# A hybrid attention and retention layer on one core: query loads of the attention's first half from ScalarE's DMA queue

## Chip, cores and metric

The kernel runs on one core of one Trainium2 chip. The metric is the time of one execution on the device in microseconds (us), as a median of runs. The core's engines are TensorE (PE, whose weight loads are listed apart as PEld), VectorE (DVE), ScalarE (ACT), GpSimd (POOL) and SyncE (SP, which computes nothing here and issues DMAs). Each takes its own stream of instructions in order; they wait for each other on semaphores.

## What is computed

One layer of a streaming encoder, for 2048 new frames of a prompt and 64 frames of a running stream with 4096 past ones. Per frame, an RMS norm and one wide input projection feed two branches: a differential attention (four heads, each query and key split into two halves of 64, causal by chunks of 64 frames) and a retention with a decaying state. Gates merge the branches and an output projection follows. The part that matters here is the attention over the prompt:

```python
def diff_attention(q, k, v, q_pos, k_pos, lam, slopes):
    s = jnp.einsum('bqhcd,bkhcd->bhcqk', q, k).astype(jnp.float32) * (DK_A ** -0.5)
    dist = jnp.abs(q_pos[:, None] - k_pos[None, :]).astype(jnp.float32)
    s = s - slopes[None, :, None, None, None] * dist[None, None, None]
    allowed = (k_pos[None, :] // CHUNK) <= (q_pos[:, None] // CHUNK)
    s = jnp.where(allowed[None, None, None], s, -jnp.inf)
    p = jax.nn.softmax(s, axis=-1)
    a = p[:, :, 0] - lam * p[:, :, 1]
    return jnp.einsum('bhqk,bkhe->bqhe', a.astype(v.dtype), v)
```

## The kernel before

**A planner writes the order.** The kernel is written as generators, one per task: the input projection's columns (`w_stream`), the attention's heads, the retention, the output. A loop (`loop`) resumes the ready task of the highest priority, and keeps an estimated clock for each engine: `P`, `A`, `V` and `G` add the estimated cost of a PE, ACT, DVE or POOL instruction to that engine's clock and return the time at which its result is there. A task that needs a result yields that time and is resumed when PE's clock has come to it. So the order in which instructions are issued to PE, ACT and DVE, and which of them stand next to each other, follows from these estimates: a changed estimate deals the order anew from that place on. The three engines keep this order as written; SP's and POOL's streams are ordered by the framework from the same program.

**Loads.** `ld` issues a DMA on SP's queue and returns an estimated landing time; `st` does the same for a store. Every DMA of the program takes one of eight semaphores, named DMAHW0_49 to DMAHW7_49 in the rows below, in turn, whichever queue it is on. Before a DMA is issued, its engine waits until the DMA that had the same semaphore, eight places earlier in the program, has landed.

**The attention.** It runs in two halves: query blocks 0 to 3 of 256 frames for all four heads, then blocks 4 to 7. For head `h` and block `p`, `load_q` fetches the query block: a buffer of 128 partitions x 4 x 256 floats (two buffers exist) is filled by four DMAs of 128 KB, one for each of the two terms (high and low part) and each half of the partitions. `q_loader` walks through heads and blocks; `load_head` fetches the keys (`K`) and values (`V`) of a head, and for the very first head also issues the first two query loads. `qk_block` makes the scores of 128 queries against the keys seen so far: two matmuls per 512 columns into a PSUM bank (L1582, L1583), which DVE moves to SBUF with the distance term added and a maximum taken (L1591, `a_acc`). `softmax` takes exponentials on ACT (L1622) and combines the two halves on DVE (L1644). `at_pv` transposes the rows on PE (L1694), casts the result to a high part on ACT (`ath`, L1708), subtracts it on DVE to get the low part (`atl`, L1710), and multiplies both with the values (L1672 to L1674). A query buffer is given back when the last score matmul of its block has run.

**What runs beside it.** The attention does not run alone: the projection's matmuls (`mm_group`, L1039) fill PE between its steps, and the retention runs beside both. A weight tile `ws` of the projection is loaded, cast on ACT (`wh`, L993) and split on POOL (`wl`, L1003). When a group of the value columns is done, ACT casts it into the buffer `thi` (L1287) and copies it to `raw` (L1289), DVE makes `tlo`, and three stores (L271) take them out. There is one buffer for `thi`, so the next such cast waits until the store of the one before has landed. Copies of other columns to `ev` (L1356) are stored to `qbT` and the like.

Of the kernel before, what the change touches and what calls it, by code (L numbers as in the profile page):

```python
# [8 lines left out]
F32 = mybir.dt.float32  # L9
# [154 lines left out]
class Hybrid:  # L164
# [97 lines left out]
        self.pool = max(self.pool, ready) + 2.4 * n + 100  # L262
        return self.pool + LAT

    def ld(self, dst, src, nbytes=0):
        self.nc.sync.dma_start(dst, src)
        self.dma = max(self.dma, self.pe) + nbytes / 300.0
        return self.dma + DMA_LAT

# [1240 lines left out]
    def load_q(self, h, p):  # L1510
        t0 = 256 * p
        yield from self.take("q")
        q = self.sb(self.ap, [128, 4, 256], "q", dt=F32R)
        for j in range(2):
            qj = self.qT[j][h, :, t0:t0 + 256].rearrange("(c d) t -> d c t", c=2)
            for o in (0, 64):
                t = self.ld(q[o:o + 64, 2 * j:2 * j + 2].bitcast(F32), qj, 1 << 17)
        self.qs.append((q, t))

    def q_loader(self, half):  # L1520
# [1374 lines left out]
```

## Time and profile before

| what | value |
|---|---|
| median of 3 runs | 1894.08 us (1893.97 to 1894.23) |
| the profiled execution's own time | 1897.48 us |
| its span, first to last instruction | 1895.5 us |
| mean granted PE clock | 0.999 |
| query loads: DMA issues, size, median to landing | 128, 128 KB, 3.7 us |
| of these in the attention's first half | 64, issued from 598.7 to 832.2 us |

The profile is of one execution, a little longer than the runs without a profile. In its lists of groups and waits an engine's name is followed by the kernel's line and by the tiles written and read; "SPq" is SyncE's queue of DMA issues, and the time of such a row is that of the issue, not of the transfer. "PE busy" includes matmuls that overlap each other, so what PE loses is best read from the waits. A DMA share of 1 means that the core's 16 DMA engines were busy all the time.

### The profile page before, as it was taken

To read this page: it belongs to the slowest core of one execution; us is meant where nothing else is said; L and a number is where in the kernel's file an instruction comes from. 1 tells how busy PE (TensorE), PEld (TensorE's weight loads), DVE (VectorE), ACT (ScalarE), POOL (GpSimd) and SP (SyncE) were. 2 spreads that over 40 slices of the span, in tenths; PEclk is the share of its full clock that TensorE was granted. 3 is DMA by queue.
4 is the path that set the end of the run, shared out by engine and by line. 5 is a ranking of instruction groups with operands and counts; after the bars stand their busy time and mean duration, and the time that the engine had idled before them with its cause. 6 is when DMAs were issued, how large, how long until landed. Compare 5 with 4: busy or idle time off the path is not lost.

```text
span 1895.5 us, 32109 instructions
## 1 busy us (share of the span) xinstructions
PE 1877.3 (99%) x10970; PEld 1649.7 (87%) x10970; DVE 1267.2 (67%) x2994; ACT 955.9 (50%) x2217; POOL 590.8 (31%) x557
## 2 busy tenths in 40 slices
PE   9999999999999899999999999999999999999999
PEld 7788888888888789888888899999999999999887
DVE  6765856657575667877577776687873329977664
ACT  6434654454434566455556555566664436654221
POOL 2420356555643132031211112211113526522442
PEclk9999999999999999999999999999999999999999
DMA  7654555565566785565523444734414748876542
GB/s 255 213 175 124 169 169 165 168 193 180 179 181 187 222 233 157 143 204 135 160 73 105 137 120 119 203 85 116 116 52 127 227 133 261 269 237 205 174 157 77
DMA packets 360581, 313.01 MB, mean 165 GB/s; under 512 B 67937, under 2 KB 310241, under 8 KB 360418
## 3 DMA queue, kind: packets, MB, share of 16 engines
q1 hardware_dynamic: 360418, 310.97, 56.0%
q8 instruction: 86, 1.41, 0.3%
q14 instruction: 77, 0.63, 0.1%
HBM read 205.43 MB, written 104.60 MB: 164 GB/s over the span
## 4 chain that ended last, share of the span: by engine, by line
PE 65%; DMA 2%; SPq 1%; DVE 1%; ACT 0%; issue 0%; POOL 0%; DVEq 0%; POOLq 0%; ACTq 0%
PE mm L1039 26%; PE at L1694 3%; PE s L1582 2%; PE s L1583 2%; PE pv L1674 2%; PE pv L1673 2%; PE pv L1672 2%; PE s L2496 1%; PE s L2498 1%; PE s L2497 1%; PE mm L2372 1%; PE at L2373 1%; PE s L2372 1%; PE s L2373 1%; PE at L2372 1%; PE s L2374 1%
## 5 line engine op out<-in xcount | busy, mean ns | idle before, releaser
L1003 POOL TENSOR_TENSOR wl<-ws,wh 128x512 fp32r<-128x512 f32 x125 | 172.5, 1396 | 360.5 <-ACT wh L993 271.8
L1039 PE MATMUL mm<-xh,wh 128*128 128x256 f32 (+2 forms) x784 | 258.4, 330 | 0.0
L1039 PE MATMUL mm<-xh,wl 128*128 128x256 f32 (+2 forms) x784 | 254.4, 324 | 0.0
L1039 PE MATMUL mm<-xl,wh 128*128 128x256 f32 (+2 forms) x784 | 254.2, 324 | 0.0
L1039 PE MATMUL mm<-wh,xh 128*128 128x512 f32 x504 | 203.3, 403 | 0.0
L1039 PE MATMUL mm<-wh,xl 128*128 128x512 f32 x504 | 197.8, 392 | 0.0
L1039 PE MATMUL mm<-wl,xh 128*128 128x512 f32 x504 | 197.6, 392 | 0.0
L1622 ACT ACTIVATE row<-row,a_mx 128x1024 f32<-128x1024 f32 (+7 forms) x144 | 149.6, 1041 | 16.4 <-DVE a_mx L1601 16.4
L1039 PEld LDWEIGHTS mm<-xh,wl 128*128 128x128 f32 x784 | 148.1, 189 | 10.3 <-POOL wl L1003 0.5
L1039 PEld LDWEIGHTS mm<-xh,wh 128*128 128x128 f32 x784 | 148.2, 189 | 9.9
L1039 PEld LDWEIGHTS mm<-xl,wh 128*128 128x128 f32 x784 | 148.4, 189 | 9.6
L1710 DVE TENSOR_TENSOR atl<-at,ath 128x512 fp32r<-128x512 f32 (+1 forms) x144 | 92.5, 659 | 80.4 <-ACT ath L1708 80.0
L1448 POOL TENSOR_TENSOR r_y<-r_y,r_sq 128x256 f32<-128x256 f32 x32 | 27.7, 865 | 360.1 <-DVE r_sq L1445 193.3
L1708 ACT CAST ath<-at 128x512 fp32r<-128x512 f32 (+1 forms) x144 | 79.4, 565 | 105.8 <-PE at L1694 103.5
L1591 DVE CUSTOM_DVE_ANT_0 row<-s,dfar 128x512 f32<-128x512 f32 (+2 forms) x150 | 93.2, 635 | 52.5 <-PE s L1583 47.6
L768 POOL TENSOR_TENSOR wl<-ws,wh 128x256 fp32r<-128x256 f32 x64 | 57.5, 899 | 190.7 <-ACT wh L759 187.1
L1039 PEld LDWEIGHTS mm<-wh,xl 128*128 128x128 f32 x504 | 94.7, 188 | 21.3
L1039 PEld LDWEIGHTS mm<-wh,xh 128*128 128x128 f32 x504 | 94.8, 188 | 17.4 <-DVE tlo L1291 0.2
L1039 PEld LDWEIGHTS mm<-wl,xh 128*128 128x128 f32 x504 | 95.0, 188 | 17.0
L1644 DVE SCALAR_TENSOR_TENSOR row<-row,a_w 128x1024 f32<-128x1024 f32 (+5 forms) x88 | 98.9, 1131 | 0.0
L993 ACT CAST wh<-ws 128x512 fp32r<-128x512 f32 x128 | 76.9, 621 | 38.6 <-DMA ws<-in_w_in_dram 25.8
L1582 PE MATMUL s<-K,q 128*128 128x512 f32 (+3 forms) x244 | 93.2, 384 | 1.3 <-DVE a_acc L1591 1.0
(497 smaller groups left out, 5441.3 us busy)
## 6 DMA issues: line engine op xcount, KB each, us to landing
ws<-in_w_in_dram SPq DMA_DIRECT2D x160, 256.0 KB, 3.5
q<-qT SPq DMA_DIRECT2D x128, 128.0 KB, 3.7
K<-kT SPq DMA_DIRECT2D x48, 256.0 KB, 4.3
V<-vN SPq DMA_DIRECT2D x24, 512.0 KB, 5.2
row<-in_x_prompt_dram SPq DMA_DIRECT2D x16, 512.0 KB, 4.4
wz<-in_w_in_dram SPq DMA_DIRECT2D x32, 256.0 KB, 4.3
row<-in_cache_k_T_dram SPq DMA_DIRECT2D x32, 256.0 KB, 3.5
row<-in_cache_v_diff_dram SPq DMA_DIRECT2D x32, 256.0 KB, 3.1
```

Of the source, the lines that this page charges most:

```text
L768: nc.gpsimd.tensor_sub(l[:, cs], src, h[:, cs].bitcast(F32))
L993: self.nc.scalar.copy(h, st)
L1003: self.nc.gpsimd.tensor_sub(l, st, h.bitcast(F32))
L1039: nc.tensor.matmul(ps, p, q, start=c == 0 and i == 0, stop=c == KC - 1 and i == 2)
L1582: nc.tensor.matmul(ps, q1s, kk, start=True, stop=False)
L1591: nc.vector.tensor_tensor_reduce(out=row[:, k0:k0 + n], in0=ps, in1=tab, scale=-SLOPES[h], scalar=3.0e38, op0=ALU.add, op1=ALU.min, accum_ ...
L1622: nc.scalar.activation(u, u, AF.Exp, bias=mx, scale=-1.0, accum_out=lp[:, k:k + 1])
L1644: nc.vector.scalar_tensor_tensor(out=u0, in0=u1, scalar=w[:, 0:1], in1=u0, op0=ALU.mult, op1=ALU.add)
L1694: nc.tensor.transpose(at[:, w:w + 128], src, self.ident)
L1708: nc.scalar.copy(ah[:, :w], at[:, :w])
L1710: nc.vector.tensor_sub(al[:, :w], at[:, :w], ah[:, :w].bitcast(F32))
L2372: nc.tensor.matmul(ps, wh[:, u, csl], oh, start=kt == 0, stop=False)
```

## The change

`ld` takes a queue, and `load_q` passes ScalarE's for blocks 0 to 3, that is for the attention's whole first half, and SyncE's for blocks 4 to 7. For each of the moved DMAs the planner's ACT clock is set to at least PE's and advanced by 165 + 435 = 600 ns.

```diff
--- before.py
+++ after.py
@@ -262,8 +262,8 @@
         self.pool = max(self.pool, ready) + 2.4 * n + 100
         return self.pool + LAT
 
-    def ld(self, dst, src, nbytes=0):
-        self.nc.sync.dma_start(dst, src)
+    def ld(self, dst, src, nbytes=0, queue=None):
+        (queue or self.nc.sync).dma_start(dst, src)
         self.dma = max(self.dma, self.pe) + nbytes / 300.0
         return self.dma + DMA_LAT
 
@@ -1511,10 +1511,13 @@
         t0 = 256 * p
         yield from self.take("q")
         q = self.sb(self.ap, [128, 4, 256], "q", dt=F32R)
+        queue = self.nc.sync if p > 3 else self.nc.scalar
         for j in range(2):
             qj = self.qT[j][h, :, t0:t0 + 256].rearrange("(c d) t -> d c t", c=2)
             for o in (0, 64):
-                t = self.ld(q[o:o + 64, 2 * j:2 * j + 2].bitcast(F32), qj, 1 << 17)
+                t = self.ld(q[o:o + 64, 2 * j:2 * j + 2].bitcast(F32), qj, 1 << 17, queue)
+                if p < 4:
+                    self.A(0, self.pe, 435)
         self.qs.append((q, t))
 
     def q_loader(self, half):
```

The number of instructions of every kind stays the same on PE, DVE and POOL; ACT has 64 DMA issues more and SP 64 fewer. Since the planner's estimates change with the first moved load, the order on PE, ACT and DVE differs from there until about the last quarter of PE's stream, which is the same again. Behind the change's added lines the numbers are higher by 3: L1582 is L1585, L1622 is L1625, L1708 is L1711.

Three places follow. In the rows, `[waits ...]` names the semaphores that the instruction waits for.

SyncE, where the attention begins: `K`, `V` and `q` are keys, values and queries, `dfar` is a table of distances, `ws` a weight tile, `qbT<-ev` a store. Before:

```order
L266 DMA q<-qT_58 64x2x256 [waits DMAHW0_49]
L266 DMA q<-qT_58 64x2x256 [waits DMAHW1_49]
L271 DMA qbT<-ev 128x256 [waits DMAHW2_49,Activation_49]
L266 DMA ws<-in_w_in_dram 128x512 [waits DMAHW3_49,Pool_49]
L266 DMA q<-qT_57 64x2x256 [waits DMAHW4_49]
L266 DMA q<-qT_57 64x2x256 [waits DMAHW5_49]
L266 DMA q<-qT_58 64x2x256 [waits DMAHW6_49]
L266 DMA q<-qT_58 64x2x256 [waits DMAHW7_49]
L266 DMA ws<-in_w_in_dram 128x512 [waits DMAHW0_49,Pool_49]
L266 DMA dfar<-in_c_dfar_dram 128x1920 [waits DMAHW1_49]
L266 DMA V<-vN_61 128x8x128 [waits DMAHW2_49]
L266 DMA V<-vN_62 128x8x128 [waits DMAHW3_49]
```

and with the change:

```order
L266 DMA K<-kT_60 64x1024 [waits DMAHW3_49]
L266 DMA ws<-in_w_in_dram 128x512 [waits DMAHW6_49,Pool_49]
L266 DMA ws<-in_w_in_dram 128x512 [waits DMAHW7_49,Pool_49]
L271 DMA qbT<-ev 128x256 [waits DMAHW0_49,Activation_49]
L266 DMA dfar<-in_c_dfar_dram 128x1920 [waits DMAHW1_49]
L266 DMA V<-vN_61 128x8x128 [waits DMAHW2_49]
L266 DMA V<-vN_62 128x8x128 [waits DMAHW3_49]
```

The query loads are gone from between `ws`, `qbT`, `dfar` and `V`; the eight semaphores still go round over both queues.

ScalarE, some instructions later, about the third query load. Before:

```order
L993 COPY wh<-ws 128x512 [waits DMAHW3_49,PE_49,Pool_49] x2
L1622 ACTIVATE row,a_lp<-row,a_acc 128x128 [waits DVE_49] x2
L993 COPY wh<-ws 128x512 [waits DMAHW0_49,PE_49,Pool_49]
L1622 ACTIVATE row,a_lp<-row,a_acc 128x256 [waits DVE_49] x2
L1622 ACTIVATE row,a_lp<-row,a_acc 128x384 [waits DVE_49]
L1356 COPY ev<-mm 128x320 [waits DMAHW4_49,PE_49,Activation_49]
L1622 ACTIVATE row,a_lp<-row,a_acc 128x384 [waits DVE_49]
L993 COPY wh<-ws 128x512 [waits DMAHW0_49,Pool_49]
```

and with the change:

```order
L993 COPY wh<-ws 128x512 [waits PE_49,Pool_49]
L993 COPY wh<-ws 128x512 [waits DMAHW6_49,PE_49,Pool_49]
L1625 ACTIVATE row,a_lp<-row,a_acc 128x128 [waits DVE_49] x2
L266 DMA q<-qT_57 64x2x256 [waits DMAHW7_49,DMAHW3_49,PE_49]
L266 DMA q<-qT_57 64x2x256 [waits DMAHW1_49]
L266 DMA q<-qT_58 64x2x256 [waits DMAHW3_49]
L266 DMA q<-qT_58 64x2x256 [waits DMAHW5_49]
L1625 ACTIVATE row,a_lp<-row,a_acc 128x256 [waits DVE_49]
L993 COPY wh<-ws 128x512 [waits DMAHW7_49,PE_49,Pool_49]
L1625 ACTIVATE row,a_lp<-row,a_acc 128x384 [waits DVE_49]
L1356 COPY ev<-mm 128x320 [waits DMAHW4_49,PE_49,Activation_49]
L1625 ACTIVATE row,a_lp<-row,a_acc 128x256
```

The four DMAs of the third load stand between the exponentials of the first pair of query blocks. The second waits on DMAHW1, which `dfar` had, the third on DMAHW3, which the second `V` load had, and the fourth on DMAHW5, which a store `qbT<-ev` had. On PE, between the first score matmul and the first that needs the third load, there stood five groups of three 512-wide projection matmuls and three groups of three 320-wide ones; now there stand three of the former and four of the latter.

ScalarE, about the first casts of attention rows. Before:

```order
L1708 COPY ath<-at 128x384 [waits PE_49]
L1287 COPY thi<-mm 128x512 [waits PE_49]
L1289 COPY raw<-mm 128x512 [waits DMAHW6_49,DMAHW5_49]
L1622 ACTIVATE row,a_lp<-row,a_mx 128x640 [waits DVE_49,Activation_49]
L1404 COPY r_o<-pv 128x256 [waits PE_49]
L1406 ACTIVATE r_sq<-r_o 128x256 [waits Activation_49]
L1408 ACTIVATE r_hi<-r_o 128x256
L1622 ACTIVATE row,a_lp<-row,a_mx 128x640 [waits DVE_49]
L1622 ACTIVATE row,a_lp<-row,a_mx 128x768 [waits DVE_49]
L1287 COPY thi<-mm 128x512 [waits DMAHW4_49,PE_49]
L1289 COPY raw<-mm 128x512 [waits DMAHW7_49]
L1708 COPY ath<-at 128x512 [waits PE_49]
```

and with the change:

```order
L266 DMA q<-qT_58 64x2x256 [waits DMAHW1_49]
L1287 COPY thi<-mm 128x512 [waits PE_49]
L1289 COPY raw<-mm 128x512 [waits DMAHW7_49]
L1625 ACTIVATE row,a_lp<-row,a_mx 128x640 [waits DVE_49]
L1625 ACTIVATE row,a_lp<-row,a_mx 128x768 [waits DVE_49,Activation_49]
L266 DMA q<-qT_57 64x2x256 [waits DMAHW4_49,DMAHW5_49,DMAHW3_49,PE_49]
L266 DMA q<-qT_57 64x2x256 [waits DMAHW6_49]
L266 DMA q<-qT_58 64x2x256 [waits DMAHW0_49]
L266 DMA q<-qT_58 64x2x256 [waits DMAHW2_49]
L1711 COPY ath<-at 128x384 [waits PE_49]
L1625 ACTIVATE row,a_lp<-row,a_mx 128x768 [waits DVE_49]
L1287 COPY thi<-mm 128x512 [waits DMAHW5_49,PE_49,Activation_49]
```

The first `ath` (128x384) stood ahead of both `thi`; it now stands behind one of them and behind the fourth and fifth query loads (of the fourth, its last DMA is the first row here), and ahead of the second `thi`. The second pair's `ath` (128x512), which stood right behind the second `thi` and `raw`, now stands behind the third.

## The prediction

> **What bounds the kernel now.** I read the page first, then the busy time by stage, then the weight loads' waits in the stage that the change touches, then the chain of waits there.
>
> ```profile
> span 1895.5 us, 32109 instructions
> PE 1877.3 (99%) x10970; PEld 1649.7 (87%) x10970; DVE 1267.2 (67%) x2994; ACT 955.9 (50%) x2217; POOL 590.8 (31%) x557
> ```
>
> TensorE (PE) is busy 99% of the span; its work is the same before and after, so the change can only move the few microseconds in which PE waits. Where these lie is shown by the busy time in stretches (columns: stretch, its length, busy time of PE, of weight loads, VectorE, ScalarE, GpSimd, granted clock, DMA share, GB/s):
>
> ```profile
> 598.00:700.00 102.00, 94.09 (x559) 82.73 (x559) 57.19 (x184) 52.63 (x134) 18.64 (x15) 0.98 0.86 236
> 700.00:800.00 100.00, 100.00 (x652) 90.77 (x651) 77.82 (x245) 58.69 (x151) 18.59 (x17) 1.00 0.56 157
> 800.00:900.00 100.00, 100.00 (x592) 88.30 (x591) 77.45 (x221) 57.42 (x141) 21.35 (x18) 1.00 0.60 171
> ```
>
> The moved loads are issued between 598.7 and 832.2 us. In that stretch PE idles 7.9 us (102.00 - 94.09), all of it before 700; from 700 to 900 it idles 0. What a weight load (PEld) waited for in 598 to 700 us (total us, times, longest):
>
> ```profile
> PEld pv L1672 <- ACT ath L1708: 3.1, 1, 3.1
> PEld tp L1582 <- issue: 2.9, 1, 2.9
> PEld s L1582 <- DVE a_acc L1591: 1.3, 2, 0.8
> PEld pv L1674 <- DVE atl L1710: 1.3, 2, 0.7
> PEld s L1583 <- DMA q<-qT: 0.8, 1, 0.8
> PEld tp L1583 <- DMA q<-qT: 0.7, 1, 0.7
> ```
>
> That is 10.1 us in all, in two large stalls. The chain of waits from 596 to 640 us says what each stands on (start us, us, what):
>
> ```profile
> 606.67 1.30 SPq L266
> 608.02 7.59 DMA V<-vN
> 615.63 0.57 SPq L266
> 616.24 3.66 DMA q<-qT
> ...
> 630.04 0.60 SPq L266
> 630.74 5.43 DMA vN<-thi
> 636.25 0.58 ACT thi L1287
> ```
>
> Stall B (about 616.9 to 619.9 us): PE needs the third query load. Its next-to-last piece is issued at 615.63, when the V load that began at 608.02 has landed (608.02 + 7.59 = 615.61): a DMA waits until the one eight places ahead of it has landed. Stall A (about 635 to 638): PE needs the cast `ath`; it stands on ScalarE (ACT) behind the cast `thi`, which waits until the store of the `thi` before it has landed; and that store left SyncE's queue (SPq) at 630.74, right behind a query load:
>
> ```profile
> 624.61 6.04 SPq L266 DMA_DIRECT2D q<-qT x4
> 630.74 0.54 SPq L271 DMA_DIRECT2D vN<-thi  x1
> 636.25 0.58 ACT L1287 CAST thi<-mm 128x512 fp32r<-128x512 f32 x1 [6.00 <-DMA vN<-thi]
> 637.21 0.99 ACT L1708 CAST ath<-at 128x512 fp32r<-128x512 f32 x2
> ```
>
> **The change, part by part.** What moves: 16 query loads of 4 DMAs, 64 issues, from SyncE's stream into ScalarE's. Their cost before:
>
> ```profile
> L266 SPq DMA_DIRECT2D q<-qT x64: 573/605/4092, 598.7 to 832.2; - x64
> 598.73 2.55 SPq L266 DMA_DIRECT2D q<-qT x4
> 602.44 3.08 SPq L266 DMA_DIRECT2D q<-qT x4
> ```
>
> SyncE is relieved of 64 x 0.605 = 38.7 us; ScalarE takes them on. PE feels neither directly.
>
> Stall A. After the change the store of `thi` has no query load ahead of it on its queue, and in the new ScalarE order the first pair's `ath` stands ahead of the second `thi`. I let the wait go: 3.1 us, half of the 1.3 us on `atl` (two waits, one of them here), and the clock that it costs:
>
> ```profile
> 635.00:640.00 5.00, 2.01 (x10) 1.59 (x10) 2.55 (x4) 3.68 (x9) 0.00 (x0) 0.90 0.86 280
> 640.00:650.00 10.00, 10.00 (x45) 8.53 (x45) 7.42 (x21) 4.53 (x10) 0.73 (x1) 0.88 0.66 204
> ```
>
> A granted clock of 0.88 over the 10 us behind the stall is 1.2 us. A: 3.1 + 0.65 + 1.2 = 4.95 us gained. Bounds: 0 (ScalarE comes as late as the store did) to 4.95.
>
> Stall B. V no longer has eight query issues ahead of it (2.55 + 3.08 = 5.6 us), but the DMA engines are full there:
>
> ```profile
> 598.00:605.00 7.00, 7.00 (x55) 7.00 (x55) 0.00 (x0) 0.80 (x2) 1.15 (x1) 1.00 1.05 235
> 605.00:610.00 5.00, 4.66 (x33) 4.23 (x32) 1.29 (x8) 2.49 (x7) 2.54 (x2) 1.00 1.10 301
> 610.00:615.00 5.00, 4.43 (x22) 3.94 (x23) 3.84 (x15) 2.22 (x7) 1.29 (x1) 1.00 1.16 313
> ```
>
> With a DMA share over 1 the same bytes cannot land 5.6 us sooner; I take a quarter, 1.4 us. The order of the change shows that the third load's later pieces still wait for V and for a store behind it, so B stays; and PE reaches it with less work done, two groups of three 512-wide matmuls fewer and one group of three 320-wide more. Six 512-wide ones take
>
> ```profile
> 620.99 1.38 PE mm L1039 x6
> ```
>
> so 0.23 us each, 0.144 for 320 by width: 1.38 - 3 x 0.144 = 0.95 us less. B: 1.4 - 0.95 = 0.45 gained. Bounds: from the whole stall gone, 2.9 + 0.7 = 3.6 gained, to 1.4 lost if V comes no sooner and ScalarE stands still meanwhile. What stands behind it on ScalarE then is exponentials and a weight cast whose users come later than the third load, so I cost ScalarE's pause at nothing; without that cover it would cost the length of B again.
>
> The wait of 1.3 us on `a_acc` is VectorE's: unchanged (bound 1.3 gained).
>
> ScalarE's added time. A group of four takes 2.55 us; the planner charges 4 x (165 + 435) ns = 2.4 us of it, so it places PE's work for that, and 0.15 us are unforeseen. What hides it is ScalarE's idle time: 58.69 and 57.42 us busy of each 100 us, and ahead of the casts that PE needs next:
>
> ```profile
> ACT ath L1708 <- PE at L1694: 12.9, 10, 3.3
> ```
>
> 12.9 us in 10 waits from 700 to 900 us, 1.29 us each. The DMA eight places ahead of a query load is mostly old there. The DMA issues from 700 to 835 us (groups with count, KB each, median us to landing; 19 rows, 122 issues):
>
> ```profile
> ws<-in_w_in_dram SPq DMA_DIRECT2D x17, 256.0 KB, 3.3
> q<-qT SPq DMA_DIRECT2D x32, 128.0 KB, 3.7
> ...
> kbT<-ev SPq DMA_DIRECT2D x1, 128.0 KB, 3.3
> ```
>
> One in 1.1 us on the mean, eight in 8.9, against a landing of 3.7: ScalarE seldom waits there. The trace has no DMA issued from ScalarE; the nearest row bounds one at 0.573 to 4.092 us, and I take SyncE's median of 0.605. For casts that come late behind a group, the first pair's above all, which now has two groups ahead of it, I allow 1.0 us lost (bounds 0 and 20, the slower rival below).
>
> [...]
>
> The second half keeps its loads on SyncE, but its order is dealt anew as well: PE's waits in 1000 to 1200 us are few,
>
> ```profile
> PEld tp L1582 <- DVE a_acc L1591: 1.9, 1, 1.9
> PEld s L1582 <- DVE a_acc L1591: 0.9, 1, 0.9
> ```
>
> and 0 is taken, between 2.8 gained and 2.8 lost.
>
> Sum: - 4.95 (A) - 0.45 (B) + 1.0 (casts) = - 4.4 us. The profiled execution took 1897.48 us, of which the span is 1895.5, and the median of the runs is 1894.08; 3.4 less. The 4.4 taken off the span is 1891.1, off the median 1889.7 us.
>
> **Rivals.** *The waits come back (no change), 1893 us.* ScalarE is stopped in B until V has landed, works off its backlog, issues two more groups and comes to the first pair's `ath` as late as `thi` did before. For it: the issues run in order on the engine that makes the cast, and in the new order eight of them stand ahead of it. Beside them some 15 casts and exponentials stand there, at 0.58 us for one like the `thi` above 8.7 us, with eight issues at 0.645 (2.55 + 0.03 over four) 5.2 more: 13.9 us of ScalarE's time. Against: some 70 of PE's matmuls stand between the third load's first use and that cast's use, at most 16 us at 0.23 each. The margin is 2 us by estimate. Without it A gives 0 to 1.5 of its 4.95: about 1 us gained, 1893.
>
> *ScalarE's issues are dear (slower), about 1900 us.* Four issues stop ScalarE; PE feels what exceeds the 0.15 us and the 1.29 us of idle time ahead of a cast. With x us for an issue the excess per group is 4(x - 0.605) + 0.15 - 1.29, so it decides from x = 0.89 us. At 1.05 us it is 0.64 us per group, 10.2 us over 16 groups; less the 4.4 it is 5.8 lost: 1899.9. At 1.2 us it would be 19.8 lost in the groups. For it: issues under load took up to 4.09 us, and from 700 to 900 PE has no idle time that could absorb any. Against: nearly all of the 64 took 0.57 to 0.61.
>
> [...]
>
> That the change does nothing is excluded: the order shows the 64 DMAs in ScalarE's stream.
>
> **How the numbers follow.** Within 0.2% (3.8 us) a measurement of this kernel cannot well tell a change from none. Faster by more: 0.43, the forecast with A gone; within: 0.29, the waits that come back; slower by more: 0.28, dear issues or stalls dealt anew behind 700 us. Predicted: 1889.7. With all of A, B and `a_acc` gone it is 4.95 + 3.6 + 1.3 = 9.85 less, 1884.2: the low end. The high end is 1899, short of the slower rival's 1899.9, whose price is a middle. The forecast's own range is 1884.2 to 1890.2.
>
> **What would show it.** A: no wait of PE for `ath` near 636, and PE clock 1.00 behind it. B: PE still waits about 3 us for the third load, whose last pieces ScalarE issues when V has landed. Casts: an issue on ScalarE of 0.57 to 0.65 us, and PE idle below 1.5 us from 700 to 900. I am wrong if issues take 0.9 us or more, if PE waits for ACT in many places behind 700, or if a wait for `ath` of 2 us or more stands near 632 us.

## Result and the profile after

| | before | changed |
|---|---|---|
| median, first comparison (22 runs each) | 1894.30 us (1892.63 to 1899.19) | 1897.45 us (1894.08 to 1901.45) |
| ratio, 95% interval | | 1.0016 (1.0009 to 1.0022) |
| median, second comparison (27 and 11 runs) | 1893.10 us | 1894.83 us |
| ratio, 95% interval | | 1.0013 (1.0004 to 1.0022) |
| profiled execution, first and second | 1897.48, 1892.77 us | 1895.78, 1893.97 us |

The change makes the kernel slower by 2 to 3 us. That lies in the range of the forecast and within 0.2%, but the forecast's direction, 4.4 us faster, was wrong.

The two first profiles stand the other way round than the medians: that of before took 3.2 us more than its median of 1894.30, that of after 1.7 us less than its own. Whoever compares them alone finds a gain. So each kernel was profiled once more. The second profile of before took 1892.77 us, where its 11 runs have a median of 1892.72: it is the one to read. Both profiles of after lie below their medians, and the second is the fastest of its 11 runs, so what the slower executions of the changed kernel lose besides is in neither.

The page of after, first profile, whose span is 1894.0 us:

```profile
PE 1878.2 (99%) x10970; PEld 1649.5 (87%) x10970; DVE 1272.1 (67%) x2994; ACT 952.5 (50%) x2217; POOL 586.9 (31%) x557
```

What PE's weight loads waited for from 598 to 700 us (total us, times, longest), after, first profile:

```profile
PEld tp L1586 <- DMA q<-qT: 3.2, 1, 3.2
PEld tp L1585 <- issue: 2.3, 1, 2.3
PEld mm L1039 <- ACT ev L1356: 2.2, 1, 2.2
```

after, second profile:

```profile
PEld tp L1586 <- issue: 2.5, 1, 2.5
PEld tp L1585 <- issue: 2.3, 1, 2.3
PEld mm L1039 <- ACT ev L1356: 2.0, 1, 2.0
```

and before, second profile:

```profile
PEld tp L1582 <- issue: 3.0, 1, 3.0
PEld s L1582 <- DVE a_acc L1591: 1.7, 3, 0.8
PEld pv L1672 <- ACT ath L1708: 1.1, 1, 1.1
PEld pv L1674 <- DVE atl L1710: 1.0, 2, 0.5
PEld s L1583 <- DMA q<-qT: 1.0, 1, 1.0
PEld tp L1583 <- DMA q<-qT: 0.7, 1, 0.7
```

Three things are to be seen. Stall A, the wait for `ath`, is gone with the change, as forecast; but in the execution of before that took the median's time it is 1.1 us and not 3.1. Stall B, the wait for the third query load (`tp` L1582/L1583, now L1585/L1586), has grown from 3.0 + 0.7 to 4.8 or 5.5 us. (`s` and `tp` are PSUM buffers of scores; `issue` stands where the profile names no releaser for the weight load, and in both kernels the matmul behind the first of these weight loads waits for the query load.) And a new wait of 2 us for a cast to `ev` has appeared.

Busy time by stretch (columns as in the prediction: stretch, length, PE, weight loads, VectorE, ScalarE, GpSimd, granted clock, DMA share, GB/s). Before, first profile, about stall A:

```profile
625.00:650.00 25.00, 22.01 (x107) 18.50 (x106) 14.98 (x43) 11.71 (x27) 0.73 (x1) 0.93 0.89 241
```

Before, second profile:

```profile
598.00:625.00 27.00, 22.47 (x136) 20.09 (x135) 10.00 (x43) 10.59 (x28) 5.35 (x5) 1.00 1.01 259
625.00:650.00 25.00, 24.01 (x136) 20.36 (x135) 16.07 (x48) 13.61 (x32) 2.01 (x2) 1.00 0.97 279
700.00:1000.00 300.00, 299.83 (x1817) 266.79 (x1816) 217.93 (x641) 167.98 (x398) 54.85 (x48) 1.00 0.49 144
```

after, second profile:

```profile
598.00:625.00 27.00, 21.04 (x117) 19.40 (x116) 6.67 (x34) 9.31 (x27) 5.43 (x5) 0.87 1.07 264
625.00:650.00 25.00, 25.00 (x137) 21.42 (x136) 15.01 (x45) 10.71 (x25) 2.02 (x2) 1.00 0.96 268
700.00:1000.00 300.00, 299.16 (x1800) 264.77 (x1798) 214.80 (x626) 164.31 (x396) 56.32 (x48) 1.00 0.52 148
```

Between the second profiles, PE idles 1.4 us more before 625, 1.0 less up to 650, 0.6 less up to 700 and 0.7 more from 700 to 1000. What is new is the clock: 0.87 over 27 us is 3.5 us at the full rate. Over all runs of the second comparison the mean clock is 0.9989 before (27 runs) and 0.9980 after (11 runs); 0.0009 of 1893 us is 1.7 us, of the 2.4 us between the means of their times (1893.18 and 1895.55). A good part of the loss is thus PE working at a lower clock behind its waits, not the waits alone.

How B came about is in the chain of waits of after, first profile (start us, us, what):

```profile
600.95 6.36 DMA q<-qT
607.33 0.51 SPq L266
607.89 8.66 DMA V<-vN
616.56 0.63 ACTq L266
617.24 4.17 DMA q<-qT
```

V's second load is issued at 607.89, 0.13 us sooner than before (608.02), since V's first load now waits until a piece of the second query load has landed (607.31), which stands eight DMAs ahead of it. V then takes 8.66 us instead of 7.59, and the third load follows it as before.

The second profiles show it otherwise. In that of before, V's second load begins at 607.67 and lands 7.54 us later, at 615.2, and the last piece of the third load begins at 615.84. In that of after, V is not on the chain of waits: a store `qbT<-ev` begun at 610.18 lands at 614.52, and the last piece of the third load begins at 614.54, 1.3 us sooner, but takes 6.46 us instead of 3.65. Before and after:

```profile
615.84 3.65 DMA q<-qT
```

```profile
614.54 6.46 DMA q<-qT
```

In both pairs of profiles the third load is complete 1.5 us later than before (621.41 against 619.90, 621.00 against 619.49), whether its last piece began later or sooner. From 615 to 620 and from 620 to 625 us the DMA share is 1.02 and 1.04 in the second profile of after and 0.86 and 0.89 in that of before; which of the transfers beside it holds the load up was not tried.

The issues themselves were priced right (group of ScalarE's DMA issues: ns min/median/max, first and last start):

```profile
L266 ACTq DMA_DIRECT2D q<-qT x64: 581/617/2052, 596.2 to 872.3; - x64
```

The new wait stands on ScalarE's order (ScalarE's timeline of after: start, duration, in brackets the idle time before):

```profile
599.22 5.34 ACTq L266 DMA_DIRECT2D q<-qT  x4
604.60 0.70 ACT L1356 COPY ev<-mm 128x256 f32<-128x256 f32 x2 [5.35 <-issue]
```

The four issues of the second load last from 599.22 to 604.56, because DMAs eight places ahead of them have not landed (the second is held until 600.95, by a load of `K` begun at 596.48 that takes 4.45 us); the two casts behind them start at 604.60, and PE, which needs the bank that they empty, stands for 1.94 us, until 605.03.

### The profile page after: what moved, and what is told of

Its sections match the earlier page's. It is cut to its first block, busy times and chain, and to the rows that moved or that the text cites. A ratio compares the mean times of both kernels' runs of the same rounds, so it can differ in the third digit from the quotient of the medians.

```text
span 1894.0 us, 32107 instructions
## 1 busy us (share of the span) xinstructions
PE 1878.2 (99%) x10970; PEld 1649.5 (87%) x10970; DVE 1272.1 (67%) x2994; ACT 952.5 (50%) x2217; POOL 586.9 (31%) x557
## 4 chain that ended last, share of the span: by engine, by line
PE 65%; DMA 2%; DVE 0%; ACT 0%; POOL 0%; issue 0%; SPq 0%; ACTq 0%; DVEq 0%; POOLq 0%
PE mm L1039 27%; PE at L1697 3%; PE s L1585 3%; PE s L1586 2%; PE pv L1677 2%; PE pv L1676 2%; PE pv L1675 2%; PE s L2499 1%; PE s L2501 1%; PE s L2500 1%; PE mm L2375 1%; PE at L2376 1%; PE s L2375 1%; PE s L2376 1%; PE at L2375 1%; PE s L2377 1%
## 5 line engine op out<-in xcount | busy, mean ns | idle before, releaser
L1625 ACT ACTIVATE row<-row,a_mx 128x1024 f32<-128x1024 f32 (+7 forms) x144 | 149.8, 1042 | 17.8 <-DMA row<-vbN 4.7
L1711 ACT CAST ath<-at 128x512 fp32r<-128x512 f32 (+1 forms) x144 | 78.9, 564 | 125.2 <-PE at L1697 118.9
L1594 DVE CUSTOM_DVE_ANT_0 row<-s,dfar 128x512 f32<-128x512 f32 (+2 forms) x144 | 88.4, 625 | 23.2 <-PE s L1586 19.3
L1356 ACT COPY ev<-mm 128x256 f32<-128x256 f32 (+2 forms) x86 | 38.7, 451 | 116.4 <-PE mm L1039 76.6
L1585 PE MATMUL s<-K,q 128*128 128x512 f32 (+3 forms) x247 | 93.7, 381 | 0.0
```

What stands on the lines that cost most here:

```text
L1356: nc.scalar.copy(ev, ps)
L1585: nc.tensor.matmul(ps, q1s, kk, start=True, stop=False)
L1594: nc.vector.tensor_tensor_reduce(out=row[:, k0:k0 + n], in0=ps, in1=tab, scale=-SLOPES[h], scalar=3.0e38, op0=ALU.add, op1=ALU.min, accum_ ...
L1625: nc.scalar.activation(u, u, AF.Exp, bias=mx, scale=-1.0, accum_out=lp[:, k:k + 1])
L1711: nc.scalar.copy(ah[:, :w], at[:, :w])
```

## Experiments

All ratios are to the kernel before, run beside each on the same chip; the forecast's own names A (wait for `ath`) and B (wait for the third load) are kept.

**Queue and order apart.** The two kernels again:

> The kernel before, unchanged, to get a second profile and the granted clock of each single run. All theories expect a ratio of 1.000. Clock theory (stalls of PE of 2 to 3 us bring a stretch of about 3.4 us at half clock in some executions, 1.7 us each, and the change has more of them): the mean granted clock lies at 0.9985 or above and the faster runs show the higher clock, about 1.7 us for 0.0009. Against it: the clock is the same as the changed kernel's (0.998) and the time does not go with it.

> The changed kernel, unchanged, to get a second profile. All theories expect a ratio of about 1.0016 (1897 us). Clock theory: its mean granted clock is some 0.001 lower than that of the kernel before, and this profile, unlike the first one with its single interval, shows two or three intervals at half clock, each right behind a stall of PE in 604 to 650 us. If the cost is PE idle time behind 700 us instead, the clock is alike and the loss of some 3 us is spread over 700 to 900.

Measured: 0.9998 (0.9989 to 1.0007) and 1.0013 (1.0004 to 1.0022). The profiles are those above. The clock's part holds; the loss from 700 to 1000 us is there too, but small.

The order without the queue, and the queue without the order:

```diff
# e2_order_only
-        queue = self.nc.sync if p > 3 else self.nc.scalar
+        queue = self.nc.sync
# e3_queue_only
-                if p < 4:
-                    self.A(0, self.pe, 435)
```

> The planner's charge of 600 ns for each of the 64 loads stays, so the order on PE, ACT and DVE is that of the changed kernel, but all loads are issued from SyncE. Theory (ScalarE stands still in its DMA issues while it waits for transfers eight places back, and PE waits for the casts behind them): the wait at 605 us is gone, the time is 1893 to 1895. Rival (the newly dealt order costs): 1897 or more, as with the change.

> The 64 loads are issued from ScalarE, but the planner is not charged for them, so the order is that of the kernel before. Theory (ScalarE stands still in its DMA issues): 1897 to 1901, with PE waiting for ACT casts at 600 to 620 us at least as long as with the change. Rival (the newly dealt order costs): 1893 to 1895.

Measured: the order alone 1.0017 (1.0008 to 1.0026), 1896.39 us; the queue alone 1.0056 (1.0043 to 1.0068), 1903.23 us; before beside them 1893.10. Neither theory is right by itself. The new order costs all of the 3 us without a single DMA on ScalarE. The queue costs 10 us in the old order, and in the new one nothing that can be told: 1894.83 us with it, 1896.39 without, with overlapping intervals. In e2 the wait for `ev` is gone, as the theory said. But B is 4.8 us (4.2 + 0.6) here too, with no query load on ScalarE: the load lands at 618.7, and PE comes to it sooner: it does nothing from 614.30 to 617.70, while in the first profile of before its last matmul ahead of the load starts at 616.17. And other waits have come (two of PE's waits, 598 to 700 us):

```profile
PEld tp L1585 <- issue: 4.2, 1, 4.2
PEld s L2042 <- DMA row<-qbT: 1.8, 1, 1.8
```

What ScalarE's queue does in an order without room for it is plain in e3. ScalarE's timeline, one wait of PE, and the chain of waits:

```profile
682.47 2.20 ACTq L266 DMA_DIRECT2D q<-qT  x3
684.72 0.40 ACT L1623 ACTIVATE row<-row,a_acc 128x128 f32<-128x128 f32 x1 [4.34 <-issue]
```

```profile
PEld at L1695 <- DVE row L1645: 4.0, 1, 4.0
```

```profile
677.05 6.37 DMA q<-qT
```

Three issues follow from 682.47 on, and one of them waits for a query load begun at 677.05 that lands at 683.42; ScalarE computes nothing for 4.34 us, and the exponentials, the combination on VectorE (L1645) and the transposes on PE (L1695) are late in turn: PE stands for 4.0 us.

**Other deals of the order.** Two more charges with all loads on SyncE (435 replaced by 150 and 600), and three kernels in which charge and queue go together for a part of the loads (e5: all but head 0's first two; e6: head 0 only; e7: heads 1 to 3 only):

```diff
# e13, e15
-        queue = self.nc.sync if p > 3 else self.nc.scalar
+        queue = self.nc.sync
...
-                    self.A(0, self.pe, 435)
+                    self.A(0, self.pe, 150)
# e5; e6 has the same effect with (p > 3 or h > 0), e7 with (p > 3 or h == 0)
-        queue = self.nc.sync if p > 3 else self.nc.scalar
+        queue = self.nc.sync if p > 3 or (h == 0 and p < 2) else self.nc.scalar
...
-                if p < 4:
+                if queue is self.nc.scalar:
```

> All loads on SyncE, the planner charged 165 + 150 = 315 ns for each of the 64 in place of 600, so the order is dealt anew in another way. Theory (any new deal costs some us against the order before, since that one happens to have few waits): slower than before by 2 to 10 us. Rival (the loss belongs to the order of the 600 ns charge alone): within 1 us of before.

> All loads on SyncE, the planner charged 165 + 600 = 765 ns for each of the 64. Theory (any new deal costs some us): slower than before by 2 to 10 us. Rival (the loss belongs to the order of the 600 ns charge alone): within 1 us of before.

> As the changed kernel, but the first two query loads (head 0, blocks 0 and 1), which fall into the full DMA engines at 598 to 604 us, stay on SyncE and cost the planner nothing; the other 56 DMAs stay on ScalarE with the charge. Theory (ScalarE's stop in those two loads keeps PE from a free bank at 605 us for 2 us): that wait is gone and the time falls from 1895-1897 to 1893-1895. Rival (the loss is in the newly dealt order and not in that stop): 1895 to 1897, with other waits in its place.

> Only the 16 DMAs of head 0 are moved to ScalarE and charged; heads 1 to 3 stay on SyncE. Theory (the loss lies where the attention begins: the wait at 605 us and the longer wait for the third load, with PE at half clock behind it): as the changed kernel, 1895 to 1897, and waits of PE before 650 us that sum to 7 us or more. Rival (the loss lies in the small waits from 700 to 1000 us of heads 1 to 3): 1893 to 1894.

> Only the 48 DMAs of heads 1 to 3 are moved and charged; head 0, with the beginning of the attention, is as in the kernel before. Theory (the loss lies at the beginning): 1892.5 to 1894, within 0.1% of before. Rival (the loss lies in heads 1 to 3): 1895 to 1897, PE idle for 2 us or more from 700 to 1000.

| kernel | ratio | 95% interval | median us |
|---|---|---|---|
| e2, charge 435, SyncE | 1.0017 | 1.0008 to 1.0026 | 1896.39 |
| e13, charge 150, SyncE | 1.0046 | 1.0033 to 1.0059 | 1902.36 |
| e15, charge 600, SyncE | 1.0026 | 1.0017 to 1.0035 | 1898.91 |
| e5 | 1.0043 | 1.0029 to 1.0057 | 1902.93 |
| e6 | 1.0030 | 1.0019 to 1.0042 | 1898.96 |
| e7 | 1.0051 | 1.0038 to 1.0064 | 1903.51 |

Every one of six deals is slower than the order before (beside them 1893.10, 1893.45 or 1893.47 us), by 3 to 10 us; in the three with no DMA moved, as expected of e13 and e15, it is 3.3, 8.9 and 5.5 us. The three expectations that placed the loss (e5, e6, e7) all failed: taking charge and queue from a part of the loads deals a further order, with waits of its own (in e5 one of 4.8 us for `ath`, in e7 one of 2.6). So a place can be told only with the order held still, as in the rest of the runs.

**The changed order held, fewer loads moved.** The charge stays on all 64:

```diff
# e9; in e10 (p > 3 or h == 0)
-        queue = self.nc.sync if p > 3 else self.nc.scalar
+        queue = self.nc.sync if p > 3 or (h == 0 and p < 2) else self.nc.scalar
```

> The planner's charges and so the order on PE, ACT and DVE are those of the changed kernel; only the first two loads (8 DMAs, 598 to 604 us) are issued from SyncE, the other 56 from ScalarE. Theory (ScalarE's stop in the second load holds the cast of ev and so PE at 605 us): that wait of 2 us is gone, the rest as with the change: 2 us faster than the changed kernel, a ratio to before of 1.0003 to 1.0008. Rival (in this order PE comes sooner to the third load and waits there for what it gained): the wait for the third load grows by as much, ratio 1.0015.

> The order of the changed kernel; head 0's 16 DMAs on SyncE, the 48 of heads 1 to 3 on ScalarE. Theory (from head 1 on the 48 issues are hidden, since the planner made room for them): as the kernel with this order and all loads on SyncE, a ratio to before of 1.0017, PE's waits from 700 to 900 us as there. Rival (the issues on ScalarE cost PE in heads 1 to 3 too): ratio of 1.003 or more.

Measured: e9 1.0008 (0.9999 to 1.0016), e10 1.0018 (1.0009 to 1.0026). In e9 no wait for `ev` is left, but those for the third load are 3.9 and 2.3 us instead of 2.3 and 2.5: PE comes sooner and stands there longer. The gain of about 1 us against the change (1.0008 against 1.0013 to 1.0016) is not certain. In e10 the 48 issues of heads 1 to 3 cost nothing that can be told beside e2's 1.0017, as its theory said.

**The clock.** Windows of 3.4 us of the second profile of after, about its two stretches at half clock:

```profile
600.70:604.10 3.40, 1.66 (x12) 1.39 (x11) 0.00 (x0) 0.70 (x2) 0.00 (x0) 1.00 1.11 230
604.10:607.50 3.40, 3.40 (x18) 3.40 (x18) 0.00 (x0) 0.00 (x0) 0.00 (x0) 0.50 1.06 248
617.80:621.20 3.40, 0.41 (x2) 0.28 (x2) 0.00 (x0) 2.47 (x7) 1.26 (x1) 0.99 0.95 220
621.20:624.60 3.40, 3.40 (x11) 3.11 (x12) 2.28 (x13) 0.92 (x2) 0.00 (x0) 0.50 1.07 247
```

Behind a window in which PE was busy for 0.41 or 1.66 us comes one of the same length at a clock of 0.50. To test this, matmuls on ones were put into the wait for the third load, once (e11), and in e8 a second time too, in the block's other column part, where nothing waits (`fill` issues them):

```diff
# e11; e8 has (b == c == 0), and so 34
+                third = h == 0 and p == 2 and b == c == ci == 0
+                if third:
+                    self.fill(7)
                 nc.tensor.matmul(ps, q1s, kk, start=True, stop=False)
+                if third:
+                    self.fill(10)
                 nc.tensor.matmul(ps, q2s, kk, start=False, stop=True)
```

> The changed kernel with 17 matmuls on ones added in PE's stream, 7 ahead of the first and 10 ahead of the second score matmul that wait for the third query load; their result is not used, and they fit into the two waits there (about 1.5 of 2.0 us and 2.1 of 2.6 to 3.2 us at 0.21 us each). Theory (a PE that stands for most of some 5 us is granted half its clock for the next 3.4 us, 1.7 us lost): no half-clock stretch at 621 us, mean clock 0.001 higher, 1 to 2 us faster than the changed kernel. Rival (the clock drops for another reason): the stretch stays, and the time is the same or up to 1 us longer.

> The changed kernel with 17 matmuls on ones added, 7 ahead of the first and 10 ahead of the second score matmul that wait for the third load, once (the kernel before this one had them a second time behind the waits, 3.8 us of added work). Theory (PE standing for most of 5 us is what brings the half clock): no half-clock stretch, and a time 1 to 2 us below the changed kernel's, 1893.5 to 1895.5. Rival (what the clock gains is lost to the added matmuls): 1895 to 1898.

The same two windows in e8:

```profile
617.80:621.20 3.40, 2.32 (x21) 2.12 (x19) 0.00 (x0) 2.49 (x9) 1.27 (x1) 1.00 0.83 212
621.20:624.60 3.40, 2.76 (x24) 2.79 (x25) 0.43 (x2) 2.57 (x8) 1.27 (x1) 1.00 0.97 286
```

The half clock is gone at this place in both kernels (in e11 the clock is 1.00 from 615 to 625 us), and e8 runs at a mean clock of 0.9996 (5 runs). The time, though, is 1.0041 (1.0028 to 1.0054) and 1.0048 (1.0036 to 1.0060): the theory of the clock holds at this place, the gain does not come. In e8 the second set of matmuls is 3.8 us of work by itself, and PE waits anew for `ath` (1.6 us) and for `tlo` (1.3 us). In e11 the clock is lower elsewhere, 0.93 from 625 to 650 us and 0.99 from 700 to 1000, so that its mean is 0.998, the changed kernel's; and a stop of ScalarE took more than the clock gave. Its timeline, and the DMA that the last of the issues waited for:

```profile
631.32 8.24 ACTq L266 DMA_DIRECT2D q<-qT  x4
639.61 0.48 ACT L1721 CAST ath<-at 128x384 fp32r<-128x384 f32 x1 [9.21 <-DMA q<-qT]
```

```profile
629.90 9.06 DMA out_v_prompt_dram<-raw
```

The fifth query load waits for a store that takes 9.06 us, and `ath` behind it is 6.1 us later than in the second profile of after (633.54): A is back with 3.8 us. There the last three of these issues took 1.91 us. The order on PE, ACT and DVE is the changed kernel's in both, but SyncE's is not: in e11 a table's load (`row`) stands ahead of the stores of `thi` and `raw`, in the changed kernel behind them. So neither kernel tests the clock alone, and the stop is not shown for the changed kernel.

PE need not be idle throughout: in the second profile of after, the window from 600.70 to 604.10 had 1.66 us of work, and half clock followed. The 5 us in the two expectations is the author's estimate; what the traces show are windows of 3.4 us.

**What B stands on.** V's two loads of head 0 issued from GpSimd (e12, order of before), or issued behind the third query load, in the order of before (e16) and of the change (e17), with the planner's estimates as they were:

```diff
# e12
+                    for o in (0, 4):
+                        tv = self.ld(v[:, o:o + 4].bitcast(F32), vj[:, o:o + 4], 1 << 18, self.nc.gpsimd)
...
# e16, e17: in load_head, and at the end of load_q
+                    self.dma = max(self.dma, self.pe) + (1 << 19) / 300.0
+                    tv = self.dma + DMA_LAT
+                    self.late.append((v, vj))
...
+        for v, vj in self.late if p == 2 else ():
+            self.nc.sync.dma_start(v.bitcast(F32), vj)
```

> The kernel before, in its order on PE, ACT and DVE, but the values of head 0 are loaded by four DMAs of 256 KB from GpSimd's queue in place of two of 512 KB from SyncE's, so that they take none of the eight semaphores that the query loads take in turn. Theory (the third query load's last pieces wait for V only because V stands eight places ahead): they are issued before V has landed, the wait of 3.5 us at 616 to 620 us falls to 1 us or less, and the time by 2 to 3 us, to 1890 to 1891.5. Rival (the DMA engines are full there, so the load lands as late by sharing them with V): the issue is earlier but the wait stays, time 1892 to 1894. Third case: GpSimd's own work of issuing holds the weight splits, 1894 or more.

> The kernel before, same order on PE, ACT and DVE; only head 0's two loads of V are issued behind the third query load instead of ahead of the stores and weight tiles before it. Theory (the third load's last pieces wait for V because V is eight places ahead, and V takes 7.6 to 8.7 us of full DMA engines): they are issued earlier, the wait of 3.5 us before 620 us falls to 1 us or less, time 2 to 3 us below before. Rival (the DMA engines are full with other transfers anyway): the wait keeps 2 us or more and the time is within 1 us of before; and if V then lands too late for the first values' matmul near 635 us, a new wait stands there.

> The changed kernel with the same move of V behind the third query load. Theory: its wait of 4.6 to 5.3 us before 621.5 us falls to 2 us or less, no half-clock stretch at 621 us, time 4 to 6 us below the changed kernel's, about 1890 to 1892. Rival: the wait stays, the time is the changed kernel's.

Measured: e12 1.0024 (1.0015 to 1.0033), e16 1.0004 (0.9995 to 1.0013), e17 1.0016 (1.0007 to 1.0025). In e12 the last piece of the second query load takes 6.53 us and lands at 612.76, and PE waits 3.2 us for it, against 1.0 in the second profile of before: a new wait. A weight split on GpSimd starts only at 617.05, and behind it leave a weight tile on SyncE, at 618.38, and the third query load, at 618.81 instead of 613.58. The third case would look like this, but the chain of waits has PE's matmuls, until 617.02, ahead of the split, and that the issues of V held it is not shown. So the theory was not put to the test there. In e17 the third load's last piece, with V now issued right behind it, takes 9.23 us to land, and B is 7 us. e16 is the telling one: B is gone without rest, and A has taken its place. Its waits of PE, SyncE's timeline and ScalarE's:

```profile
PEld pv L1681 <- ACT ath L1717: 5.2, 2, 4.9
```

```profile
621.73 6.85 SPq L266 DMA_DIRECT2D q<-qT  x4
628.67 0.54 SPq L271 DMA_DIRECT2D vN<-thi  x1
```

```profile
634.06 0.59 ACT L1287 CAST thi<-mm 128x512 fp32r<-128x512 f32 x1 [7.83 <-DMA vN<-thi]
635.02 0.99 ACT L1717 CAST ath<-at 128x512 fp32r<-128x512 f32 x2
```

The store of `thi` lands at 634 whether PE was held up by B (633.8 in the second profile of before) or not, since the fourth query load's issues, 6.85 us long, stand ahead of it. What PE gains at B it loses at A.

**What A stands on.** Only the first three stores of `thi` behind the attention's beginning are issued from ScalarE, in the kernel before (e18) and together with V behind the third load (e19):

```diff
+            act = getattr(self, "far", False) and getattr(self, "few", 3) > 0
+            self.few = getattr(self, "few", 3) - act
-            self.give("thi", self.rows_out(self.vN[0][t0:t0 + rt, gsl], hi.bitcast(F32), nu, nh << 16))
+            self.give("thi", self.rows_out(self.vN[0][t0:t0 + rt, gsl], hi.bitcast(F32), nu, nh << 16,
+                                           nc.scalar if act else None))
```

> The kernel before, order unchanged on PE and DVE; only the first three stores of thi behind the attention's beginning are issued from ScalarE, so that none stands behind a query load on SyncE. Theory (the wait for ath near 636 us stands on that store's place in SyncE's queue): the store is issued 2 to 3 us earlier, the wait of 1.1 us is gone, time 1 to 1.5 us below before. Rival (until about 636 us the full DMA engines set the time, so what one wait gives another takes): thi lands as late, time within 0.7 us of before.

> V of head 0 behind the third query load and the three stores of thi from ScalarE, both in the order of the kernel before. Theory (store's place in the queue): of the 4.65 us wait for ath some 3 go, the wait for the third load stays gone, time 1890 to 1892, below both kernels. Rival (full DMA engines until 636 us): a wait of 3 us or more remains between 620 and 640 us, time 1893 to 1895.

Measured: e18 0.9997 (0.9988 to 1.0006), 1892.74 us; e19 0.9986 (0.9977 to 0.9995), 1890.11 us, against 1893.52 beside them. ScalarE's timeline of e18:

```profile
625.35 0.35 ACTq L271 DMA_DIRECT2D vN<-thi  x1
632.47 0.59 ACT L1287 CAST thi<-mm 128x512 fp32r<-128x512 f32 x1 [1.25 <-PE mm L1039]
```

The store leaves at 625.35, 4.0 us before its time in the second profile of before (629.35), the next `thi` waits for PE and no longer for the store, and no wait for `ath` is left. So the place in SyncE's queue was A's cause, as the forecast had it; what that is worth by itself, 0.8 us between the medians, cannot be told from nothing. In e19 both go. PE's waits from 598 to 700 us:

```profile
PEld s L1596 <- DMA q<-qT: 2.1, 2, 1.2
PEld s L1595 <- DVE a_acc L1604: 1.2, 2, 0.6
PEld s L1595 <- DMA q<-qT: 1.1, 1, 1.1
PEld pv L1687 <- DVE atl L1723: 0.7, 1, 0.7
PEld tp L1596 <- issue: 0.3, 1, 0.3
```

Nothing of A is among them and of B at most the last 0.3 us; the two loads before and behind (`s` for a query load) cost 3.2 us together. And e19 is 3.4 us faster than before, and so faster than both kernels: a gain near the forecast's 4.4, from three stores and the place of two loads in place of 64 issues and a new order.

## Why the prediction was wrong

- **"A: 3.1 + 0.65 + 1.2 = 4.95 us gained" is the term that was mis-sized.** The mechanism was right: the wait is gone in both profiles of after, and e18 removes it by the store alone. But 4.95 was read off one execution that took 3.4 us more than the median of the runs. In the execution at the median A is 1.1 us of wait, half of the 1.0 on `atl` and no lost clock: 1.6 us were there to gain, and e18 gained 0.8. Between these two executions of before lie 4.7 us, of which A has 2.0 of wait and some 1.7 of clock (0.93 against 1.00 over the 25 us to 650). The prediction set the 3.4 aside as a difference between two reference times, and then subtracted the whole 4.95 from the median.
- **"0 is taken" for the order dealt anew is the step that failed.** The forecast took it for the second half alone, and for the first counted only what it could see at B, "0.95 us less". That order costs 3.3 us by itself (e2); two other deals with no DMA moved cost 8.9 and 5.5 (e13, e15). The second half was not the place: from 1000 to 1200 us PE idles 0.95 us in the second profile of before and not at all in that of after. Of e2's 3.3 us its mean clock (0.9985 over its runs, 0.9989 before) makes less than 1; in its profile PE idles 1.0 us longer from 650 to 700 and 0.9 longer from 700 to 1000 than in the second one of before.
- **B, "0.45 gained".** The 0.95 us less work ahead of it was right. "V 1.4 us sooner" failed in the first pair of profiles, where V landed 0.9 later; in the second the third load's last piece began 1.3 us sooner; but in both the third load was complete 1.5 us later, which the forecast had no term for. B grew from 3.7 to about 5 us, and PE worked at half clock behind it, which the forecast did not count. By the prediction's own terms, the sum would be 1.4 smaller were V to land no sooner, for B would grow by the 0.95: that is nearer to what came.
- **"I cost ScalarE's pause at nothing" failed**, one load earlier than where the forecast looked. It considered what stands behind the third load; the second stopped ScalarE for 5 us, with casts to `ev` behind it, and PE lost 2 us at 605. The 1.7 and 1.0 us that PE waited before for `a_acc` and for the second load were gone; the forecast had the first as unchanged and no term for the second.
- **Price of an issue: right.** 0.605 was taken, 0.617 measured, so the slower rival (from 0.89 us) falls. That the time lies within the stated range is luck, since the range's high end came from that rival. The allowance of 1.0 us for late casts and "PE idle below 1.5 us from 700 to 900" held: PE is busy for all but 1.2 and 0.4 us of that stretch in the two profiles of after.
- **"The waits come back"** has the time nearer than the forecast, but not its mechanism: no wait for `ath` came. What came true of it is that ScalarE, stopped by an issue that waits, hands the wait on to PE, at the second load (2 us) and not at this cast; e3 shows the same at 680 us, with 4.34 us of ScalarE and 4.0 of PE. Nor did the new queue bring the load sooner: in both pairs of profiles the third load was complete 1.5 us later.

Open: which of the small waits behind 650 us in each deal belong to which move, why the third load lands later with the change, why e11 loses 3.8 us of PE time from 700 to 1000, and what the changed kernel's slower executions (up to 1901.45), none of which was profiled, lose besides. These were not tried.

## What to carry to other kernels

Compare the profiled execution's time with the median first: where it is longer, its largest stall may be the surplus, and what is not in the median cannot be gained from it. A change that moves a planner's estimate deals the order anew, and in this kernel, whose PE is busy for 99%, that alone cost 3.3 to 8.9 us in three of three deals; measure it apart from what the change is about. Where two waits follow each other in one stretch with full DMA engines, try to remove them together: here one alone gave 0.8 us or nothing, both gave 3.4.

## What the runs showed of the hardware

- ScalarE's DMA issues ran beside its own work where they did not wait. In the second profile of after two issues, 1.24 us together, and an exponential of 0.83 us start together:

```profile
623.62 0.83 ACT L1625 ACTIVATE row<-row,a_mx 128x640 f32<-128x640 f32 x1 [3.36 <-DVE a_w L1636]
623.63 1.24 ACTq L266 DMA_DIRECT2D q<-qT  x2
```

  So these issues did not cost ScalarE their full time, as the planner charged it. What stopped the engine is issues that waited: for 5.34 us from 599.22 on in the first profile of after, and for 8.24 us from 631.32 on in e11.
- PE was granted half its clock in stretches of 3.41 us: in the first profile of before from 638.96 to 642.38, in that of after from 621.17 to 624.59 (0.50 in both). In the former another begins at 1895.06, 368 times 3.413 us behind the first. The stretch of the same length ahead of each had little work: PE was busy for 0.76 us from 635.55, for 0.07 us from 1891.65 (the execution's end) and, in the first profile of after, for 0.35 us from 617.76. In steps of 3.413 us counted from these, the others with less than 2.3 us of work (1.49 from 615.07, 2.21 from 618.48 and 1.92 from 1045.15 before, 1.94 from 614.35 after) are followed by full clock, and so are all with more. Windows of 3.4 us in other traces, laid by hand to end where the half clock begins: 0.00 us of work in e2, 0.41 and 1.66 in the second profile of after, 0.51 in e16, 1.16 in e18, 1.74 in e5 and 1.84 in e19 are followed by a clock of 0.50 or 0.51; 2.32 in e8, about the same place, by 1.00. So how much work keeps the clock is not shown: 1.49 us did in one place, 1.84 did not in another.
- It matters where a wait falls. In the second profile of before PE was busy for only 0.35 us from 616.20 to 619.60, and the clock is 1.00 from 615 to 625; in that of after it was busy for 0.41 us from 617.80 to 621.20, and half clock followed. The wait of 2 us for `ev` lies within one window in the second profile of after (1.66 us busy from 600.70 on, then half clock) and across two in the first (2.39 and 2.49 us busy from 600.69 on, full clock). The wait at B in the first profile of before is split over two, with 1.49 and 2.21 us busy, and the clock stays full.
